# Two MLPs by a seven-product scheme: where the last additions into the residual happen, and where two groups of buffers lie

## The chip, the cores and the metric

The kernel runs on one core of a Trainium2 chip. The metric is device time in microseconds of one execution. Engines are named as the profile names them: PE is TensorE (matrix products, results in PSUM), DVE is VectorE, ACT is ScalarE, POOL is GpSimd, SP is SyncE. Each takes its instructions in order. SP issues most DMAs; the DMAs that add into their target are issued by POOL.

## The reference, cut to what matters

A residual stream x of 1024 tokens by 1024 channels goes through two layers and a last norm:

```
for l in range(2):
    h = rmsnorm(x, norm_mix_g[l])
    x = x + mixer(h)                       # l=0: attention and S5; l=1: HGRN2, 8 heads
    h = rmsnorm(x, norm_mlp_g[l])
    x = x + square(relu(h @ w_ff_in[l])) @ w_ff_out[l]     # 4096 hidden channels
return rmsnorm(x, final_norm_g)
```

The change is about the line with the MLP, and about the places of buffers in the two stages that follow or precede it.

## The kernel before, in words

**Products.** x is kept transposed, as eight tiles `x0` to `x7` of 128 channels by 1024 tokens. Each float32 operand is split into a high part (float32r, an ACT copy, L105) and the rest (a subtraction, L106), and a product is three matmuls: high by high, low by high, high by low (L349). A product of two matrices, each cut in 2 x 2 blocks, is made from seven block products in place of eight (`seven`, L334 on), in the order 1, 6, 5, 7, 2, 3, 4. They gather in three PSUM banks `a`, `b`, `c` (each there twice). Between them ACT copies `p1` from `a` (L355), and DVE makes `vv` and `ww` from `b` (L357, L359); a function `take` fetches the four result blocks after products 7, 2, 3 and 4. Products 7 and 4 go on gathering in `b` and product 3 in `c`, so PE may write them only when DVE has read what came before.

**First matmul of an MLP (`stage1`).** `entry` scales the eight x tiles by the norm's gain (ACT, L285), writes x to DRAM (`xd`, 16 blocks of 128x512, SP) and makes the seven right-hand sides of four pairs of tiles (`combos`: sums on DVE, L263 to L271, and splits). Each of the four goes to a slot: slots 0 to 3 are pools `t0` to `t3`, slot 4 is the place of the x tiles themselves, product p in the place of `x(p-1)`. Sixteen steps then make 256 hidden channels each and write them to DRAM (`spill`).

**Second matmul (`stage2`).** Its steps u run over bands of the hidden channels: step u multiplies up to four hidden blocks (rows u-4 to u-1 as far as they exist) into the pair of x tiles q, q+4 with q = (u - npairs) mod 4. npairs is 16 in the first MLP and 14 in the second, where the last four hidden tiles are left to `tail`. In the last four steps (u from npairs to npairs+3) 4, 3, 2 and 1 hidden blocks are left, and each finishes one pair of x tiles. Every step puts its four results into z tiles (one ACT copy, L434, and three DVE differences, L436) and adds them to `xd` in DRAM by POOL DMAs (L437). After each of the last four steps the pair is loaded back (`load_x`, L456). In the first MLP `fin` then squares the pair and adds the squares up (ACT L302, DVE L304) for the next norm; after the MLP the pair is scaled and split for the mixer (`new_xg`, L108 and L109). The block in slot 4 (rows 0, 5 and 10) is used last in step 14 of either MLP.

**Left sides (`left_sides`).** For each step SP loads four weight blocks `r11` to `r22` (L314), POOL makes three sums and a difference, ACT and DVE split seven of them into the rings `wh` and `wl`.

**Tail.** The second MLP's last four hidden tiles are loaded (L496) into eight z tiles, split, and multiplied plainly into each x tile (L527, L530); then come the last norm and the stores.

**Pools.** SBUF pools are stacked from either end. In an MLP: on the left `t2` and `pv` (the ring of the left sides: `r`, `s`, `wh`, `wl`, 46 KB per partition), on the right x, `t3`, `pe` (sums: eight z, `v`, `w`, `p1`, `ac`, `ad`, 26 KB), `t1`, `t0`. In the HGRN2 mixer: on the right x, `pgb`, `pgc`, `hgc` (kept small tiles: masks, `f`, `q`, `sc`), `pga`, `pw` (weights of the projections), on the left `hg` (its working tiles: `sn`, `oh`, `ol`, `M0`, `M1`, `on`, `qd0`, `ki0`, `qd1`, `ki1`, `V`, `sg`, `kT`). A tile that comes to lie over one of the stage before waits until that one has been read for the last time. Over `pw`, the mixer's weights of the last projections, lies `t0` in the second MLP.

**Order.** A planner puts each engine's instructions in an order at build time, by the order of the program as priority and by simulated times; waits between engines and for DMAs are then put in. On the chip an engine whose next instruction waits does not take a later one.

Of the kernel before, what the change touches and what calls it, by code (L numbers as in the profile page):

```python
# [10 lines left out]
F32 = mybir.dt.float32  # L11
# [3 lines left out]
ALU = mybir.AluOpType  # L15
# [4 lines left out]
P = 128  # L20
SEQ = 1024
# [34 lines left out]
class Trunk:  # L56
# [160 lines left out]

    def open_fast(self):
        self.st_f = [ExitStack() for _ in range(6)]
        t2, self.pv, t3, self.pe, t1, t0 = (  # L220
            st.enter_context(self.pool(n, side=side))
            for st, n, side in zip(
                self.st_f, ("t2", "pv", "t3", "pe", "t1", "t0"), ("left", "left", "right", "right", "right", "right")
            )
        )
        self.tp = (t0, t1, t2, t3)
        if self.ps_stack:
            self.ps_stack.close()
        self.ps_stack = ExitStack()
        self.ps_f, self.ps_sm = (  # L230
            self.ps_stack.enter_context(self.tc.tile_pool(name=n, bufs=2, space=PSUM, reuse_waits="tile"))
            for n in ("psx", "pss")
        )
# [189 lines left out]
        put(4, b21)  # L423
        return T

    def stage2(self, src, Ts, q):

        v, gp = self.nc.vector, self.nc.gpsimd
        (x11, x12), (x21, x22) = self.xd[q], self.xd[q + 4]

        def put(x, *src):
            t = self.z()
            if len(src) == 1:
                self.nc.scalar.copy(t, *src)  # L434
            else:
                v.tensor_tensor(t, *src, ALU.subtract)  # L436
            gp.dma_start(x, t, accum_op=ALU.add)  # L437

        def take(p, a, b, c, p1, vv, ww):
            if p == 7:  # L440
                put(x22, ww, c)
            elif p == 2:
                put(x11, a)
            elif p == 3:
                put(x12, c, vv)
            elif p == 4:
                put(x21, b, p1)

        self.seven(src, Ts, take)

    def load_x(self, q):
        out = []
# [7 lines left out]
    def mlp(self, l, Ts, fin=None):  # L460

        npairs = FF // 256 - 2 * l
        spill = [
            [self.pd.tile([P, 512], F32, tag=f"sq{j}{k}", name=f"sq{j}{k}") for k in range(4)] for j in range(FF // 256)
        ]
        rows = [self.stage1(l, Ts, spill)]
        xT = [None] * ND
        at = 0  # L470
        for u in range(1, npairs + 4):
            if u < npairs:
                rows.append(self.second_row(u, spill))
            use = range(max(0, u - 4), min(npairs, u))
            size = 4 * P * P * len(use)
            src = self.io[f"wout{l}"][at : at + size].rearrange("(k p c) -> k p c", k=4, p=P)
            at += size
            q = (u - npairs) % 4
            self.stage2(src, [rows[j] for j in use], q)
            if u >= npairs:  # L480
                xT[q], xT[q + 4] = self.load_x(q)
                if fin:
                    fin(q, xT)
        return xT, spill

    def tail(self, xT, spill):
# [448 lines left out]
    def attn_load(self, h, pa, qd, kd, dv):  # L935
        nc = self.nc
        st = []
        for c in range(2):
# [5 lines left out]
            st.append((qa, qb, kk))  # L944
        V = pa.tile([P, NT, P], F32, tag="V", name="V", bufs=2)
        nc.sync.dma_start(V.rearrange("p t c -> p (t c)"), dv[h])
        return dict(V=V, st=st)

# [286 lines left out]
    def hgrn_decay(self, h, d, gate, C, pt):  # L1235

        nc = self.nc
        v = nc.vector
        f, sn = gate
        om = C["om"][:, h : h + 1]  # L1240
        qd = pt.tile([P, SEQ], F32, tag=f"qd{d}", name=f"qd{d}", bufs=2 - d)
        ki = pt.tile([P, SEQ], F32, tag=f"ki{d}", name=f"ki{d}")
        blk = lambda t: t.rearrange("p (b s) -> p b s", b=NT)
        ones = self.ones[:, 0:64]

        near, far = (slice(64, 128), slice(0, 64)) if d == 0 else (slice(0, 64), slice(64, 128))
        qb, kb, fb = blk(qd), blk(ki), blk(f)
        for b in range(NT):
            if d == 0:
                v.tensor_tensor_scan(qb[:, b, 64:128], fb[:, b, 64:128], ones, 1.0, ALU.mult, ALU.mult)  # L1250
                v.tensor_tensor_scan(kb[:, b, 0:63][:, ::-1], fb[:, b, 1:64][:, ::-1], ones[:, 0:63], 1.0, ALU.mult, ALU.mult)
            else:
                v.tensor_tensor_scan(qb[:, b, 0:64][:, ::-1], fb[:, b, 0:64][:, ::-1], ones, 1.0, ALU.mult, ALU.mult)
                v.tensor_tensor_scan(kb[:, b, 65:128], fb[:, b, 64:127], ones[:, 0:63], 1.0, ALU.mult, ALU.mult)
        e = 63 if d == 0 else 64
        nc.gpsimd.memset(kb[:, :, e : e + 1], 1.0)

        dec = pt.tile([P, NT], F32, tag="dec", name="dec", bufs=4)
        nc.gpsimd.memset(dec, 0.0)
        if d == 0:  # L1260
            v.tensor_tensor(dec[:, 1:8], qb[:, 0:7, 127], kb[:, 1:8, 0], ALU.mult)
            v.tensor_tensor(dec[:, 1:8], dec[:, 1:8], fb[:, 1:8, 0], ALU.mult)
        else:
            v.tensor_tensor(dec[:, 0:7], qb[:, 1:8, 0], kb[:, 0:7, 127], ALU.mult)
            v.tensor_tensor(dec[:, 0:7], dec[:, 0:7], fb[:, 0:7, 127], ALU.mult)
        v.reciprocal(qb[:, :, far], kb[:, :, far])
        v.reciprocal(kb[:, :, near], qb[:, :, near])
        v.scalar_tensor_tensor(ki, sn, om, ki, ALU.mult, ALU.mult)
        return qd, ki, dec

    def hgrn_inputs(self, h, xg, C, pt):

        nc = self.nc
        v = nc.vector
        base = W_ODD + 5 * h
        load = lambda j: self.load_w(base + j, nc.gpsimd)
        H = {}
        g0 = self.hgrn_gate(h, load(1), xg, C, pt)
        yield H
        g1 = self.hgrn_gate(h, load(2), xg, C, pt)  # L1280
        yield H
        d0 = self.hgrn_decay(h, 0, g0, C, pt)
        ps = self.proj(load(3), xg)
        t = pt.tile([P, SEQ], F32, tag="sn", name="t", bufs=2)
        v.tensor_tensor(t, ps, self.R, ALU.mult)
        yield H
        d1 = self.hgrn_decay(h, 1, g1, C, pt)
        ps = self.proj(load(0), xg)
        q = self.pc1.tile([P, SEQ], F32, tag="q", name="q")
        v.tensor_tensor(q, ps, self.R, ALU.mult)  # L1290
        V = pt.tile([P, SEQ], F32, tag="V", name="V")
        self.to_tokens(t, lambda j: slice(128 * j, 128 * j + 128), V, lambda p: p)
        H["V"] = V
        H["dirs"] = [d0, d1]
        for d in (d0, d1):
            v.tensor_tensor(d[0], d[0], q, ALU.mult)
        yield H
        ps = self.proj(load(4), xg)
        sg = pt.tile([P, SEQ], F32, tag="sg", name="sg")
        v.tensor_tensor(sg, ps, self.R, ALU.mult)  # L1300
        nc.scalar.activation(sg, sg, AF.Sigmoid)
        H["sg"] = sg
        yield H

    def hgrn_mix(self, h, H, C, pt):

        nc = self.nc
        v, gp = nc.vector, nc.gpsimd
        wide = lambda tag, bufs=1: pt.tile([P, SEQ], F32, tag=tag, name=tag, bufs=bufs)
        dirs, V = H["dirs"], H["V"]  # L1310
        sc = self.pc1.tile([P, NT, P], F32, tag="sc", name="sc")
        for g in range(2):
            gs = slice(4 * g, 4 * g + 4)
            for d in range(2):
                qd, ki, dec = dirs[d]
# [7 lines left out]
        for d in range(2):  # L1323
            kT = wide("on" if d else "kT")
# [125 lines left out]
@with_exitstack  # L1450
def trunk_kernel(ctx, tc, io):
    T = Trunk(ctx, tc, io)
    ctx.callback(lambda: T.ps_stack.close())
    nc = T.nc
    v = nc.vector
    T.setup()

    def load_xT():
        T.px = ctx.enter_context(T.pool("px", side="right"))
        out = []  # L1460
        for d in range(ND):
            t = T.px.tile([P, SEQ], F32, tag=f"x{d}", name=f"x{d}")
            nc.sync.dma_start(t, io["x"][d])
            out.append(t)
        return out

    mix, xT = T.mixer0(load_xT)
    for _ in T.out_proj(0, mix, PAIRED, xT):
        pass
    T.st_b.close()  # L1470
    T.st_w.close()
    T.st_m.close()
    T.open_fast()
    Ts = T.entry(xT, 16, (0, 1, 2, 3))
    acc = []

    def fin(q, x):
        if q == 0:
            acc.extend(T.half(t) for t in ("ac", "ad"))
        for d in (q, q + 4):  # L1480
            T.square_add(acc, x[d], d == 0, T.z)

    xT, _ = T.mlp(0, Ts, fin)
    T.finish_rstd(T.pc, acc)
    T.close_fast()
    T.open_hgrn()
    xg = [None] * ND
    for d in PAIRED:
        xg[d] = T.new_xg(d, xT[d], T.gcol(8, d))
    T.psum(3, 0, 2)  # L1490
    T.mixer1(xg, xT)
    T.close_hgrn()
    T.open_fast()
    Ts = T.entry(xT, 24, (1, 3, 0, 2))
    xT, spill = T.mlp(1, Ts)
    T.tail(xT, spill)

# [86 lines left out]
```

## Time and profile before

| | us |
|---|---|
| median of 3 runs | 2767.81 (2761.88 to 2770.64) |
| the profiled execution | 2766.7 |
| its span in the profile | 2764.9 |
| PE busy | 2550.8 (92%) |
| DVE busy | 1999.2 (72%) |
| ACT busy | 1059.9 (38%) |
| POOL busy | 958.1 (35%) |

The stages, from the first and last matmuls of their lines: attention and S5 mixer to 641, first MLP 641 to 1349, HGRN2 mixer 1349 to 2033, second MLP 2036 to 2685, tail from 2697. Busy time of PE is that of pipelined matmuls; what is of use is where it is idle and what ended the idle time. The granted clock (PEclk) is a share of full speed.

### The profile page before, as it was taken

The numbers are of one execution on the slowest core, as the hardware profiler recorded it, in microseconds if no ns is written. First come the engines' busy times: TensorE is split into PE (matmuls) and PEld (weight loads), VectorE is DVE, ScalarE is ACT, GpSimd is POOL, SyncE is SP. The second block draws the span as 40 slices with busy tenths as digits, with TensorE's granted clock in tenths as the row PEclk, the third lists the DMA queues.
The fourth block names the chain that finished last, engine by engine and source line by source line (L and its number), as shares of the span: only waits on it lengthen the run. The fifth ranks groups of instructions, "written<-read, shape, count | busy, mean of one in ns | idle before, by whom it ended". The sixth has DMA issues, their size and how long they took to land.

```text
span 2764.9 us, 33375 instructions
## 1 busy us (share of the span) xinstructions
PE 2550.8 (92%) x12040; PEld 2080.2 (75%) x12040; DVE 1999.2 (72%) x2868; ACT 1059.9 (38%) x1918; POOL 958.1 (35%) x759
## 2 busy tenths in 40 slices
PE   6888889998999989999799999999879999899977
PEld 5676768885788857787588888888757888677756
DVE  9788867767667678886485767666586676688845
ACT  3233346655334344443322122222163343444424
POOL 6555421231323234454222222222233232345432
PEclk8989999999999999999799999999989999999998
DMA  3222452321334257566411011111033332567672
GB/s 142 65 84 72 143 148 66 88 80 50 99 107 125 93 148 177 143 176 138 92 54 39 32 45 39 39 39 39 16 107 98 109 122 96 146 154 174 142 171 101
DMA packets 139285, 276.36 MB, mean 100 GB/s; under 512 B 16880, under 2 KB 29808, under 8 KB 139120
## 3 DMA queue, kind: packets, MB, share of 16 engines
q1 hardware_dynamic: 118384, 236.47, 26.8%
q0 software_dynamic: 20736, 37.76, 8.8%
q8 instruction: 95, 1.56, 0.2%
q14 instruction: 70, 0.57, 0.1%
HBM read 173.50 MB, written 94.37 MB: 97 GB/s over the span
## 4 chain that ended last, share of the span: by engine, by line
PE 65%; DVE 15%; issue 7%; DMA 6%; POOL 3%; ACT 2%; SPq 1%; POOLq 0%; DVEq 0%; ACTq 0%
PE big L130 19%; PE b L349 14%; PE c L349 9%; PE a L349 9%; DMA z<-sq 3%; DVE wl L106 2%; PE sm L995 2%; DVE l L106 2%; PE big L1363 1%; PE sm L130 1%; PE tail L527 1%; PE big L960 1%; PE sm L1319 1%; PE big L1334 1%; PE big L961 1%
## 5 line engine op out<-in xcount | busy, mean ns | idle before, releaser
L130 PE MATMUL big<-hi,wh 128*128 128x512 f32 x976 | 312.8, 401 | 12.8 <-ACT hi L108 11.3
L130 PE MATMUL big<-lo,wh 128*128 128x512 f32 x976 | 309.5, 396 | 9.4 <-DVE lo L109 9.4
L130 PE MATMUL big<-hi,wl 128*128 128x512 f32 x976 | 310.1, 398 | 0.0
L349 PE MATMUL b<-h,wh 128*128 128x512 f32 x672 | 271.7, 404 | 30.7 <-DVE w L359 29.4
L349 PE MATMUL b<-l,wh 128*128 128x512 f32 x672 | 269.5, 401 | 2.3 <-DVE l L106 2.3
L349 PE MATMUL b<-h,wl 128*128 128x512 f32 x672 | 269.2, 401 | 1.0 <-DVE wl L106 1.0
L105 ACT CAST wh<-s 128x512 fp32r<-128x512 f32 (+3 forms) x204 | 118.4, 583 | 356.4 <-PE b L349 160.0
L106 POOL TENSOR_TENSOR wl<-raw,wh 128x1024 fp32r<-128x1024 f32 x58 | 143.2, 2468 | 305.4 <-ACT wh L105 305.3
L105 ACT CAST wh<-raw 128x1024 fp32r<-128x1024 f32 x74 | 77.5, 1048 | 441.5 <-PE big L130 296.6
L106 DVE TENSOR_TENSOR wl<-r,wh 128x512 fp32r<-128x512 f32 (+3 forms) x279 | 220.1, 797 | 24.7 <-ACT wh L105 24.4
L106 DVE TENSOR_TENSOR l<-z,h 128x512 fp32r<-128x512 f32 x232 | 191.7, 856 | 60.5 <-ACT h L105 60.1
L130 PEld LDWEIGHTS big<-lo,wh 128*128 128x128 f32 x976 | 184.8, 190 | 52.1 <-DVE lo L109 11.1
L130 PEld LDWEIGHTS big<-hi,wh 128*128 128x128 f32 x976 | 182.8, 191 | 52.4 <-ACT hi L108 12.0
L437 POOL DMA_DIRECT2D xd<-z x144 | 127.6, 971 | 272.5 <-ACT z L434 181.0
L130 PEld LDWEIGHTS big<-hi,wl 128*128 128x128 f32 x976 | 185.6, 191 | 40.4 <-issue 0.2
L105 ACT CAST wh<-r 128x512 fp32r<-128x512 f32 (+3 forms) x279 | 159.8, 582 | 123.3 <-PE b L349 60.6
L105 ACT CAST h<-z 128x512 fp32r<-128x512 f32 x232 | 139.0, 620 | 170.0 <-DMA z<-sq 62.1
L349 PE MATMUL a<-h,wh 128*128 128x512 f32 x448 | 181.3, 405 | 14.7 <-ACT p L355 6.3
L323 POOL TENSOR_TENSOR s<-s,r 128x512 f32<-128x512 f32 (+3 forms) x68 | 107.0, 1573 | 244.4 <-DVE wl L106 243.3
L106 DVE TENSOR_TENSOR wl<-s,wh 128x512 fp32r<-128x512 f32 (+3 forms) x204 | 138.7, 681 | 71.5 <-ACT wh L105 68.2
L349 PE MATMUL c<-h,wh 128*128 128x512 f32 x448 | 180.2, 402 | 8.6 <-ACT h L105 5.4
L349 PE MATMUL a<-h,wl 128*128 128x512 f32 x448 | 180.7, 403 | 4.3 <-DVE wl L106 4.3
(430 smaller groups left out, 6007.2 us busy)
## 6 DMA issues: line engine op xcount, KB each, us to landing
raw<-w SPq DMA_DIRECT2D x74, 512.0 KB, 3.3
xd<-z POOLq DMA_DIRECT2D x144, 256.0 KB, 5.8
r<-win SPq DMA_DIRECT2D x128, 256.0 KB, 2.9
sq<-z SPq DMA_DIRECT2D x128, 256.0 KB, 2.9
z<-sq SPq DMA_DIRECT2D x128, 256.0 KB, 4.9
r<-wout SPq DMA_DIRECT2D x96, 256.0 KB, 4.6
x<-x SPq DMA_DIRECT2D x16, 512.0 KB, 6.6
xd<-x SPq DMA_DIRECT2D x32, 256.0 KB, 2.3
```

The source lines that it names most:

```text
L105: nc.scalar.copy(hi, src)
L106: (eng or nc.vector).tensor_tensor(lo, src, hi, ALU.subtract)
L130: nc.tensor.matmul(ps[:, t], a[:, s], b[:, t], start=(first and i == 0 and j == 0), stop=(last and i == n - 1 and j == 2),)
L323: gp.tensor_tensor(s2, s1, r["r11"], ALU.add)
L349: nc.tensor.matmul(bank[p], x[:, s], y, start=(p in (1, 6, 5) and i == 0 and j == 0), stop=(i == n - 1 and j == 2), skip_group_check=True,)
L437: gp.dma_start(x, t, accum_op=ALU.add)
L527: nc.tensor.matmul(ps, x[:, ks], y, start=(k == 0 and j == 0), stop=(k == 3 and j == 2))
L960: nc.tensor.matmul(S[:, ks], qa[:, qs], kk[:, ks], start=True, stop=False)
L961: nc.tensor.matmul(S[:, ks], qb[:, qs], kk[:, ks], start=False, stop=True)
L995: nc.tensor.matmul(po, wT[:, k, :], A["V"][:, k, :], start=(k == 0), stop=(k == NT - 1))
L1319: nc.tensor.matmul(ps[:, 128 * b : 128 * b + 128], ki[:, bs], qd[:, bs], start=True, stop=True)
L1334: nc.tensor.matmul(kv[:, bs], kTs[d][:, bs], V[:, bs], start=True, stop=True)
```

## The change

The last four steps of the first MLP and the last three of the second add their seven pieces to the x tiles in SBUF, on DVE, with seven additions or subtractions in place of three differences, a copy and four adding DMAs. For this the x tiles are loaded before: in the first MLP pair k before step npairs - 1 + k, in the second pairs 1 to 3 before step npairs - 2 + k, while its pair 0 still goes through DRAM in step npairs and is loaded after step npairs + 1.

In an MLP the pools `pv` and `pe` change places: `pv` lies on the right between `t3` and `t1`, `pe` on the left after `t2`. In the mixer the tiles `qd1`, `ki1`, `V`, `sg` and `kT` (4 KB each) move from `hg` on the left to `hgc` on the right. And the four pairs of the second MLP's entry go to slots 0, 3, 1, 2 in place of 1, 3, 0, 2.

```diff
     def open_fast(self):
-        t2, self.pv, t3, self.pe, t1, t0 = (
+        t2, self.pe, t3, self.pv, t1, t0 = (
...
-                self.st_f, ("t2", "pv", "t3", "pe", "t1", "t0"), ("left", "left", "right", "right", "right", "right")
+                self.st_f, ("t2", "pe", "t3", "pv", "t1", "t0"), ("left", "left", "right", "right", "right", "right")
...
-    def stage2(self, src, Ts, q):
+    def stage2(self, src, Ts, q, x=None):
...
-        self.seven(src, Ts, take)
+        def take_here(p, a, b, c, p1, vv, ww):
+            x11, x12, x21, x22 = (x[k // 2][:, 512 * (k % 2) : 512 * (k % 2) + 512] for k in range(4))
+            for y, plus, minus in {7: [(x22, ww, c)], 2: [(x11, a, None)], 3: [(x12, c, vv)], 4: [(x21, b, p1)]}.get(p, []):
+                v.tensor_tensor(y, y, plus, ALU.add)
+                if minus is not None:
+                    v.tensor_tensor(y, y, minus, ALU.subtract)
+
+        self.seven(src, Ts, take_here if x else take)
...
-            self.stage2(src, [rows[j] for j in use], q)
-            if u >= npairs:
-                xT[q], xT[q + 4] = self.load_x(q)
-                if fin:
-                    fin(q, xT)
+            for k in {npairs - 1: (0,), npairs: (1,), npairs + 1: (2,), npairs + 2: (3,)}.get(u + l, ()):
+                if l == 0 or k:
+                    xT[k], xT[k + 4] = self.load_x(k)
+            here = xT[q] is not None and u >= npairs
+            self.stage2(src, [rows[j] for j in use], q, [xT[q], xT[q + 4]] if here else None)
+            if u == npairs + 1 and l:
+                xT[0], xT[4] = self.load_x(0)
+            if u >= npairs and fin:
+                fin(q, xT)
...
-        qd = pt.tile([P, SEQ], F32, tag=f"qd{d}", name=f"qd{d}", bufs=2 - d)
-        ki = pt.tile([P, SEQ], F32, tag=f"ki{d}", name=f"ki{d}")
+        pool = self.pc1 if d else pt
+        qd = pool.tile([P, SEQ], F32, tag=f"qd{d}", name=f"qd{d}", bufs=2 - d)
+        ki = pool.tile([P, SEQ], F32, tag=f"ki{d}", name=f"ki{d}")
...
-        V = pt.tile([P, SEQ], F32, tag="V", name="V")
+        V = self.pc1.tile([P, SEQ], F32, tag="V", name="V")
...
-        sg = pt.tile([P, SEQ], F32, tag="sg", name="sg")
+        sg = self.pc1.tile([P, SEQ], F32, tag="sg", name="sg")
...
-        wide = lambda tag, bufs=1: pt.tile([P, SEQ], F32, tag=tag, name=tag, bufs=bufs)
+        wide = lambda tag, bufs=1: (self.pc1 if tag == "kT" else pt).tile([P, SEQ], F32, tag=tag, name=tag, bufs=bufs)
...
-    Ts = T.entry(xT, 24, (1, 3, 0, 2))
+    Ts = T.entry(xT, 24, (0, 3, 1, 2))
```

## Rows read from the trace of the kernel before

**Rows 1.** The page, part 1: busy us (share of the span) and instructions.

```profile
PE 2550.8 (92%) x12040; PEld 2080.2 (75%) x12040; DVE 1999.2 (72%) x2868; ACT 1059.9 (38%) x1918; POOL 958.1 (35%) x759
```

**Rows 2.** Windows: stretch, length, busy of PE, PEld, DVE, ACT, POOL, PEclk, DMA.

```profile
1278.00:1298.00 20.00, 20.00 (x87) 15.95 (x85) 10.06 (x17) 5.84 (x12) 8.07 (x10) 1.00 0.54 92
1298.00:1348.60 50.60, 30.90 (x95) 21.72 (x95) 27.33 (x40) 20.86 (x38) 16.68 (x18) 0.76 0.68 152
1348.60:1378.80 30.20, 25.62 (x111) 21.48 (x110) 13.92 (x54) 6.13 (x10) 5.56 (x20) 0.83 0.40 72
1378.80:1985.00 606.20, 605.08 (x3175) 513.42 (x3174) 416.72 (x627) 134.51 (x229) 163.39 (x102) 1.00 0.12 39
...
2646.00:2685.50 39.50, 31.29 (x121) 22.85 (x119) 18.52 (x35) 12.09 (x28) 14.59 (x19) 0.96 0.84 181
2685.50:2697.30 11.80, 0.02 (x1) 0.03 (x1) 2.63 (x5) 1.31 (x3) 2.10 (x3) 0.68 1.08 295
```

**Rows 3.** Timeline of PE, end of the first MLP: start, length, instruction, [idle before <-releaser].

```profile
1330.10 0.80 PE L349 MATMUL b<-h,wh 128*128 128x512 f32 x1 [4.93 <-DVE w L359]
...
1345.86 0.80 PE L349 MATMUL b<-h,wh 128*128 128x512 f32 x1 [6.24 <-DVE w L359]
...
1363.32 2.04 PE L152 MATMUL sm<-ones,ac 128*128 128x128 f32 x8 [4.58 <-DVE ex L568]
```

**Rows 4.** Timeline of ACT, in the same stretch.

```profile
1343.85 1.15 ACT L302 ACTIVATE z<-x 128x512 f32<-128x512 f32 x2 [6.59 <-DMA x<-xd]
```

**Rows 5.** Waits of SP's queue: waited for: us in total, times, longest.

```profile
SPq L456 <- DMA xd<-z: 86.2, 29, 9.3
```

**Rows 6.** DMA issues: count, KB each, median us from issue to landing.

```profile
xd<-z POOLq DMA_DIRECT2D x144, 256.0 KB, 5.8
...
x<-xd SPq DMA_DIRECT2D x32, 256.0 KB, 3.3
```

**Rows 7.** Lines, DVE, 1298 to 1378.8: count, busy us, mean ns, idle before.

```profile
L304 DVE TENSOR_TENSOR ac<-ac,z 128x512 f32<-128x512 f32 x7 | 4.8, 688 | 13.4 <-ACT z L302 13.4
L304 DVE TENSOR_TENSOR ad<-ad,z 128x512 f32<-128x512 f32 x7 | 4.8, 687 | 4.9 <-ACT z L302 4.9
L436 DVE TENSOR_TENSOR z<-b,p 128x512 f32<-128x512 f32 x4 | 2.7, 680 | 0.0
```

**Rows 8.** Timeline of DVE, end of the first MLP.

```profile
1302.15 2.40 DVE L106 TENSOR_TENSOR wl<-r,wh 128x256 fp32r<-128x256 f32 x1 [3.20 <-ACT wh L105]
...
1348.11 0.69 DVE L304 TENSOR_TENSOR ac<-ac,z 128x512 f32<-128x512 f32 x1
1348.72 0.69 DVE L304 TENSOR_TENSOR ad<-ad,z 128x512 f32<-128x512 f32 x1
```

**Rows 9.** Timeline of POOL, in the same stretch.

```profile
1301.89 2.38 POOL L106 TENSOR_TENSOR wl<-raw,wh 128x1024 fp32r<-128x1024 f32 x1 [1.70 <-ACT wh L105]
```

**Rows 10.** Timeline of PE, end of the second MLP and the tail's start.

```profile
2662.30 0.63 PE L349 MATMUL b<-h,wh 128*128 128x512 f32 x1 [2.86 <-DVE w L359]
...
2697.28 0.79 PE L527 MATMUL tail<-h,h 128*128 128x512 f32 x1 [11.83 <-ACT h L105]
2697.87 0.63 PE L527 MATMUL tail<-h,l 128*128 128x512 f32 x1
2698.29 0.63 PE L527 MATMUL tail<-h,wh 128*128 128x512 f32 x1
```

**Rows 11.** Timeline of ACT, end of the second MLP.

```profile
2659.96 0.62 ACT L105 CAST h<-r 128x512 fp32r<-128x512 f32 x1 [4.23 <-DMA r<-wtail]
...
2696.61 1.79 ACT L105 CAST h<-z 128x512 fp32r<-128x512 f32 x3 [5.38 <-DMA z<-sq]
```

**Rows 12.** Timeline of PE, start of the second MLP.

```profile
2036.47 0.50 PE L349 MATMUL a<-h,wh 128*128 128x512 f32 x1 [3.02 <-ACT wh L105]
2040.73 0.80 PE L349 MATMUL a<-h,wl 128*128 128x512 f32 x1 [3.75 <-DVE wl L106]
```

**Rows 13.** Lines, DVE, 2009 to 2033: count, busy us, mean ns, idle before.

```profile
L106 DVE TENSOR_TENSOR l<-z,h 128x512 fp32r<-128x512 f32 x10 | 6.4, 681 | 0.0
```

## Prediction, made before the changed kernel was seen

> **What bounds the kernel now.** I read part 1 of the page first: TensorE is busy for 92% of the span [rows 1], so a change pays only where TensorE waits or runs at its lower clock. Busy times by stretch then show where that is [rows 2]. In the long odd-layer mixer, 1378.8 to 1985 us, TensorE is busy 605.1 of 606.2 us. In the four products of the last pairs of the first MLP and the start of the mixer (1298 to 1378.8) it is busy 56.5 of 80.8 us, at a mean clock of 0.76 and 0.83. From 2646 to 2697.3, the last three pairs of the second MLP, it is busy 31.3 of 51.3 us. These two ends, and the start of the second MLP, are the places that the diff touches. The rest should stay.
>
> In the first end the reader is to see one pattern in TensorE's timeline three times: idle 4.93 and 6.24 us until VectorE has made `w` (L359), and 4.58 us before the norm's sums [rows 3]. VectorE makes `w` late because it takes its instructions in order and the square sums (L304) stand in front: they wait for ScalarE, which waited 6.59 us for the reload of x (`x<-xd`) [rows 4]. In that stretch VectorE stood 13.4 and 4.9 us before the two sums [rows 7]. The reload is late because it waits on SyncE for the adding DMA to land: 86.2 us in 29 waits [rows 5], and such a DMA takes 5.8 us, the reload 3.3 us more [rows 6]. So each of the last pairs goes PSUM, z, adding DMA, reload, square, and the other engines' queues stand behind it.
>
> In the second end the same SyncE waits hold back the loads queued behind them: TensorE stands 2.86 us, because a split of the tail's weights waits for `r<-wtail` in front of `w`, and then 11.83 us until ScalarE has the first activation [rows 10], for which ScalarE waited on `z<-sq` [rows 11].
>
> **Part 1: the last pairs are added in SBUF.** Removed: the four z copies or differences of 7 pairs (4 in the first MLP, 3 in the second; the second's first pair stays with DRAM, as its x is not loaded yet) and 28 of 144 adding DMAs. Per pair ScalarE loses one copy, VectorE gets 7 additions in place of 3 differences. The reloads stay 32 in number, but are issued one pair ahead, at a time when the last addition into that x lies three pairs back.
>
> First end. TensorE's work from 1298 to 1378.8 is 95 matmuls, then 111 of which 32 are the small ones of the norm. At full clock one costs 20.0 us / 87 = 0.23 us [rows 2]; eight small ones took 2.04 us [rows 3], the other sixteen about 2. The floor is (95 + 79) x 0.23 + 4 + 2 = 46 us, 35 less than now. VectorE comes first, though. It is busy 27.3 + 13.9 = 41.2 us there [rows 2]. The change adds 3 pairs x 4 additions and 2 for the end of the pair before, 14, at 0.60 us from start to start [rows 8]: 8.4 us, so 49.6 us, to 1347.6 if it never idles. The last `lo` (L109) must come before the last 24 matmuls of the first projection and the norm's 32: with what TensorE can do meanwhile that puts it at about 1352 where it now stands at 1378.8, 27 less. Some idling stays, since with one or two blocks a product is shorter than the copy, difference and additions around it. For its size I take the second end, where three such pairs leave TensorE idle 39.5 - 31.3 - 2.86 = 5.3 us that are not due to a load [rows 2, 10]. So **22 us**. From above 27. From below: only the 18.3 us before L304 go and the 8.4 us come on top: 10.
>
> The order of the seven sets another small wait. After product 7 TensorE may not write bank `c` before VectorE has read it; now that is one difference, afterwards the addition of `ww` stands ahead of it: 0.6 us more per pair, inside the 5.3 us kind above.
>
> Second end. TensorE's floor from 2646 is 119 x 0.23 = 27 us. VectorE is busy 18.5 + 2.6 us [rows 2]; 12 more additions are 7.2 us and the eight splits of the tail's activations, which now come after 2697, move in with 5.3 us: 33.6 us, to 2679.6. The tail then starts 17.7 us earlier, and its first 14 matmuls, now at the lower of the two clock levels (0.43 us from start to start [rows 10]), gain 14 x 0.20 = 2.8 us if there is no gap in front: 20.5. With 5 us of idling left: **16 us**. From below: only the 11.83 us and the 2.8 go, the 7.2 come: 7. Late next is VectorE's own queue, not a transfer: the z ring is no longer used by the last three pairs, so `z<-sq` can be issued while they run, and no SyncE wait for an adding DMA stands in front. After the tail's start TensorE is steadily busy up to the last norm, so what is won there reaches the end.
>
> A rule of the Trainium skill speaks against this part. The rows: a split of 128x256 took 2.40 us (1302.15), beside a 2.38 us subtraction of GpSimd that began 0.26 us before it [rows 8, 9]. The page SBUF — State Buffer (Who interferes with whom) says that a VectorE instruction with two SBUF inputs contends with a GpSimd instruction that reads SBUF, and that the loser waits for the whole instruction. Three of the seven additions (`ww`, `vv`, `p1`) have both inputs in SBUF, the differences that they replace had one in PSUM. By the rule, with GpSimd busy 16.7 of 50.6 us, a third of 21 additions would wait up to 2 us: 14 us, and the sum would be 2742. But the square sums L304 also have two SBUF inputs, and 14 of them in that stretch average 0.688 us against 0.680 us for L436, which reads PSUM [rows 7]. I keep 0.60 us.
>
> **Part 2: the places in SBUF.** At the start of the second MLP the ring of split weights (`pv`) now lies over the mixer's q and k products, which are read until its last mixing step; afterwards it lies over masks, gates and scores, read earlier. So the first weights can be loaded and split before TensorE needs them, and the 3.02 us (ScalarE's `wh`) and 3.75 us (`wl`) in front of the first two matmuls [rows 12] can go: +7. Against that the blocks' places change: (1,3,0,2) to (0,3,1,2) puts the first block into slot 0, which in both layouts lies over the mixer's projection weights, and TensorE reads these to its last projection, at 2033. Before that VectorE now does 10 splits [rows 13] and 7 sums; the first block would be stuck after its first split, with five of the eight z's, and so the second block as well. About 10 of these 17 instructions then come after 2033, 6 us in a stretch where VectorE is the last to finish. I take **+2**, from -6 to +7. At the start of the first MLP two of the seven `wl` now lie over the mixer output that the last projection reads: two splits late, **-1** (-2 to 0). In the mixer every tile keeps its size and count, only the pool differs, and TensorE has no idle time there to lose or win: 0. GpSimd's 28 issues and ScalarE's copies are off the path: 0.
>
> **Sum.** 22 + 16 + 2 - 1 = 39 us. The profiled execution took 2766.7 us (span 2764.9), 1.1 below the median of 2767.8, so I forecast 2766.7 - 39 = 2728 us. From below 10 + 7 - 6 - 2 = 9 (2758), from above 27 + 20.5 + 7 = 54.5 (2712). Its own range is 2714 to 2741.
>
> **Rivals.**
> - VectorE takes the place of the DMA. All 26 added VectorE instructions lie in stretches where it is the last, and the first block of the second MLP is stuck as above. Then the sums come near their lower ends, some 12 us: 2755 (2742 to 2759). For it: the floors above are VectorE's, not TensorE's. Against: its idle time in the first end is 80.8 - 41.2 = 39.6 us, five times what is added. Chance 0.2.
> - Slower: the wait moves onto VectorE. Its first addition of a pair waits for the reload, and the splits and `w` that TensorE needs stand behind it in order, as behind L304 now. If the reload lands after product 7 of its pair, the stalls stay, and 26 x 0.6 = 16 us come on top: 2782. It decides where the reload is less than about 8 us ahead (5.8 + 3.3). For it: three of the second MLP's reloads need the place of block 10, which the pair before still reads, and SyncE waits in order. Against: from that block's second-last use to the addition lie some 14 us of products. Chance 0.06.
> - More: with no waits left, both ends reach their floors and the second MLP starts without its two gaps: 2712 (2700 to 2714). VectorE would have to be without idle time. Chance 0.08.
> - Nothing: the stalls were set by the order in which instructions were planned, and the new plan has others of the same size, 2767 (2759 to 2775). Against: the waits named end on a transfer, not on an order. Chance 0.04.
>
> **How the numbers follow.** The forecast has 0.62. The range 2712 to 2750 holds it, half of the first rival and a part of the third, about 0.8. A measurement can tell 0.3% (8.3 us) from no change. Faster than 2759.5: 0.62 + 0.2 + 0.08 = 0.90. Same 0.04, slower 0.06.
>
> **What would show it.** Right: no SyncE wait on an adding DMA in the last pairs; no ScalarE wait for `x<-xd` before a square; TensorE's idle time between 1298 and the first gate down from 24 to under 10 us; the 11.83 us before the tail gone; the mixer still about 606 us; 116 adding DMAs. Wrong: an addition in SBUF that begins after a reload lands with TensorE idle behind it; the mixer longer by more than 3 us; or at the second MLP's start VectorE's queue ending later than now by more than 6 us.

## The result and the profile after

The changed kernel takes 2722.4 us (median of 4 runs, 2720.0 to 2727.5) where the kernel before takes 2765.2: ratio 0.9846, 95% interval 0.9821 to 0.987. The profiled execution took 2724.6 us (span 2722.8). The forecast was 2728. Its sum was right to 3 us, but not its terms, as this table shows. It cuts both spans at the same matmuls, counted from the start of each stage. The third column is the forecast, the rest are the differences to the kernel before (us), each from one profiled execution; "additions only" and "places only" are the runs with one part of the change each.

```
stretch (in the trace before)                    length  forecast  changed  additions only  places only
start to stage 2 of the first MLP, 0-983.4        983.4      +1      -5.8        +0.6          -5.1
steps 1 to 14 of stage 2, 983.4-1251.2            267.8       0      -0.5        +0.6          -1.2
steps 15 and 16, 1251.2-1290.4                     39.2       0      +5.2        +6.2          -0.7
steps 17 to 19, mixer's start, 1290.4-1378.8       88.4     -22     -16.4       -15.5          -3.2
the mixer, 1378.8-2033.1                          654.3       0      -0.9        +0.5          +0.9
start of the second MLP, 2033.1-2104.2             71.1      -2      -2.7        +0.9          -4.0
rest of its stage 1, 2104.2-2380.2                276.1       0      -5.1         0.0          -5.2
steps 1 to 14 of its stage 2, 2380.2-2644.6       264.3       0      -0.1        -0.4          -4.7
step 15 to the end, 2644.6-2764.9                 120.3     -16     -15.7       -15.1          -2.9
sum                                                         -39     -42.0       -22.2         -26.1
```

Three rows carry what was not foreseen: 11 us gained in the two rows with a stage 1, where the change adds and removes no instruction, and 5 us lost in steps 15 and 16. The page, part 1, beside [rows 1]: VectorE has 28 instructions more, GpSimd 28 fewer, as counted.

```profile
PE 2527.8 (93%) x12040; PEld 2077.1 (76%) x12040; DVE 2018.5 (74%) x2896; ACT 1055.8 (39%) x1911; POOL 921.4 (34%) x731
```

The windows, beside [rows 2] (stretch, length, busy time of PE, PEld, DVE, ACT, POOL with instructions, granted clock, DMA share, GB/s): first end, mixer, the last steps before the tail's first matmul, and the rest of those steps.

```profile
1289.30:1361.30 72.00, 58.13 (x236) 44.84 (x235) 59.06 (x118) 29.98 (x48) 14.66 (x25) 0.88 0.13 44
1361.30:1967.00 605.70, 604.56 (x3174) 513.41 (x3173) 411.84 (x621) 130.03 (x225) 160.62 (x101) 1.00 0.13 41
2618.20:2650.10 31.90, 25.52 (x97) 19.42 (x95) 18.75 (x36) 10.98 (x25) 6.16 (x9) 0.89 0.81 246
2650.10:2674.00 23.90, 22.75 (x96) 17.77 (x97) 17.87 (x30) 8.35 (x15) 0.00 (x0) 1.00 0.11 34
```

TensorE's timeline in the first end has no 4.93, 6.24 and 4.58 us any more [rows 3]. In their place stand short waits for VectorE, in each of the last two pairs for `v` and for `w`.

```profile
1305.77 0.49 PE L349 MATMUL a<-h,wh 128*128 128x512 f32 x1 [1.83 <-ACT wh L105]
...
1319.42 0.50 PE L349 MATMUL b<-h,wh 128*128 128x512 f32 x1 [2.87 <-DVE v L357]
1323.82 0.80 PE L349 MATMUL b<-h,wh 128*128 128x512 f32 x1 [2.29 <-DVE w L359]
...
1332.47 0.50 PE L349 MATMUL b<-h,wh 128*128 128x512 f32 x1 [2.58 <-DVE v L357]
1336.07 0.80 PE L349 MATMUL b<-h,wh 128*128 128x512 f32 x1 [2.64 <-DVE w L359]
```

VectorE's timeline ahead of the second of these (`w`, 1323.09) shows why. Nothing in it is idle; what TensorE waits for stands at the end of a queue of splits and square sums.

```profile
1318.69 0.68 DVE L357 TENSOR_TENSOR v<-b,p 128x512 f32<-128x512 f32 x1
1319.29 0.28 DVE L106 TENSOR_TENSOR wl<-r,wh 128x128 fp32r<-128x128 f32 x1
1319.49 0.68 DVE L304 TENSOR_TENSOR ad<-ad,z 128x512 f32<-128x512 f32 x1
1320.09 0.68 DVE L304 TENSOR_TENSOR ac<-ac,z 128x512 f32<-128x512 f32 x1
1320.69 1.27 DVE L109 SCALAR_TENSOR_TENSOR lo<-x,vec,hi 128x1024 fp32r<-128x1024 f32 x1
1321.89 0.68 DVE L304 TENSOR_TENSOR ad<-ad,z 128x512 f32<-128x512 f32 x1
1322.49 0.68 DVE L304 TENSOR_TENSOR ac<-ac,z 128x512 f32<-128x512 f32 x1
1323.09 0.68 DVE L359 TENSOR_TENSOR w<-b,p 128x512 f32<-128x512 f32 x1
```

SyncE's waits for an adding DMA, 86.2 us in 29 before [rows 5], are halved, not gone; 116 adding DMAs are left of 144 [rows 6].

```profile
SPq L464 <- DMA xd<-z: 49.4, 15, 8.0
```

At the second end the 2.86 and 11.83 us [rows 10] are replaced by one 4.70 and one 1.46, and the tail's first products now run between the last pairs' own.

```profile
2637.58 0.51 PE L349 MATMUL a<-h,wh 128*128 128x512 f32 x1 [4.70 <-ACT wh L105]
2639.55 0.80 PE L349 MATMUL b<-h,wh 128*128 128x512 f32 x1 [1.46 <-DVE w L359]
2647.71 0.49 PE L349 MATMUL a<-h,wh 128*128 128x512 f32 x1 [0.18 <-ACT p L355]
2650.14 0.49 PE L539 MATMUL tail<-h,h 128*128 128x512 f32 x1
```

### The profile page after: what moved, and what is told of

The parts are those of the page before. It is cut to its first block, busy times and chain, and to the rows that moved or that the text cites. A ratio compares the mean times of both kernels' runs of the same rounds, so it can differ in the third digit from the quotient of the medians.

```text
span 2722.8 us, 33307 instructions
## 1 busy us (share of the span) xinstructions
PE 2527.8 (93%) x12040; PEld 2077.1 (76%) x12040; DVE 2018.5 (74%) x2896; ACT 1055.8 (39%) x1911; POOL 921.4 (34%) x731
## 4 chain that ended last, share of the span: by engine, by line
PE 60%; DVE 20%; DMA 8%; issue 6%; ACT 2%; POOL 2%; SPq 1%; POOLq 0%; DVEq 0%; ACTq 0%
PE big L130 21%; PE b L349 11%; PE c L349 7%; PE a L349 7%; DMA z<-sq 5%; DVE wl L106 3%; DVE l L106 3%; PE sm L1007 2%; PE sm L130 1%; PE big L1376 1%; PE tail L539 1%; PE big L972 1%; PE sm L1332 1%; PE big L1347 1%; DMA xd<-z 1%
## 5 line engine op out<-in xcount | busy, mean ns | idle before, releaser
L323 POOL TENSOR_TENSOR s<-s,r 128x512 f32<-128x512 f32 (+3 forms) x68 | 98.7, 1452 | 255.1 <-DVE wl L106 254.0
L349 PE MATMUL c<-l,wh 128*128 128x512 f32 x448 | 177.1, 395 | 4.4 <-DVE l L106 4.4
L330 POOL TENSOR_TENSOR s<-s,r 128x512 f32<-128x512 f32 (+3 forms) x68 | 88.8, 1305 | 273.1 <-DVE wl L106 217.4
```

What stands on the lines that cost most here:

```text
L323: gp.tensor_tensor(s2, s1, r["r11"], ALU.add)
L330: gp.tensor_tensor(s2, s2, r["r12"], ALU.add)
L349: nc.tensor.matmul(bank[p], x[:, s], y, start=(p in (1, 6, 5) and i == 0 and j == 0), stop=(i == n - 1 and j == 2), skip_group_check=True,)
```

## The experiments

The runs after a point are made to answer it; each is the changed kernel with the edit shown, unless it says "the kernel before". Ratios are to the kernel before, timed on the same chip; the changed kernel has 0.9846.

### 1 and 2: the two parts apart

```diff
# additions only: the kernel before with stage2 and mlp of the changed kernel
# places only: the changed kernel with stage2 and mlp of the kernel before
```

> The kernel before with the additions in SBUF and the earlier reloads alone; pools and block places as before. Theory (the adding DMA out of the queues is what pays, at the first and the second end): 31 of the 42 us come, 16 at the first end and 15 before the tail, so 2766 - 31 = 2735 us (2730 to 2740). Rival (the places in SBUF bring most of it, by letting loads start earlier): 2750 us or more. In the trace, by the theory, the 11.83 us before the tail and the waits of ScalarE for the reload are gone as after the whole change.

> The changed kernel with the additions put back into DRAM and the reloads back behind their pair; pools and block places stay changed. Theory: only the start and the first stage of the second MLP gain, 3 + 5 us, and the two ends stand as before: 2766 - 8 = 2758 us (2754 to 2763). Rival (places bring most): 2740 us or less. Nothing (places alone do nothing): 2766.

Measured: additions only 2745.0 us, 0.9934 (0.9918 to 0.995); places only 2742.9 us, 0.9926 (0.9907 to 0.9945). Both expectations were wrong, the theory's and the rival's. Each part brings about half, and within the intervals the two add up to the whole. The additions bring 15 us at either end, as in the whole change, and lose 6 us in steps 15 and 16. The places bring 5 us in each row with a stage 1, 5 in the second MLP's stage 2, and 3 to 4 at the start and the ends. So the places act also where TensorE never waits.

The windows of one such stretch say how. These are 740 to 930 us, the first MLP's stage 1, of the kernel before, additions only, places only and the changed kernel. TensorE is busy for all 190.00 us at full granted clock in each, and does 817, 816, 830 and 830 matmuls.

```profile
740.00:930.00 190.00, 190.00 (x817) 153.06 (x816) 130.45 (x185) 73.88 (x123) 55.39 (x38) 1.00 0.38 114
```

```profile
740.00:930.00 190.00, 190.00 (x816) 153.18 (x816) 130.47 (x186) 73.88 (x123) 55.94 (x38) 1.00 0.38 114
```

```profile
740.00:930.00 190.00, 190.00 (x830) 155.53 (x829) 132.09 (x189) 74.53 (x125) 56.55 (x39) 1.00 0.37 116
```

```profile
740.00:930.00 190.00, 190.00 (x830) 155.43 (x829) 132.11 (x188) 74.81 (x126) 57.30 (x39) 1.00 0.38 114
```

The same matmuls follow each other faster: 233.2 ns apart before, 229.3 after (means of all starts under 245 ns apart in both MLPs). A pair here is one step: seven products of four blocks, three matmuls each, 84 in all. The intervals repeat to 1 or 2 ns from pair to pair at the same place in the pair. Matched with the addresses of the compiled program, which stand in no trace, they go with where the operands lie: 226 or 227 ns for most where weights and moving block (the activations that stream past them) both lie on the right, mostly 231 to 238 where they lie on different sides. Two things differ between the sides: the region, and the start. Tiles on the left start at a multiple of 128 B, those on the right 96 B past one. The pads of runs 5, 6, 7 and 9 below bear the difference of 96 B out.

### 3 and 4: two steps of the prediction

```diff
-    Ts = T.entry(xT, 24, (0, 3, 1, 2))
+    Ts = T.entry(xT, 24, (1, 3, 0, 2))
```

> The changed kernel with the order of block places (1,3,0,2) instead of (0,3,1,2) at the entry of the second MLP. The prediction's step (the first block in place 0 waits for the last projection's weights and costs up to 6 us): about 2718 us, with splits of the first block before the last projection ends. Rival (the splits come late because the plan puts them behind the last addition to x, whatever their place): 2721 to 2725 us, no change. Third (place 0 for the first block is the better one in the new layout): 2728 us or more.

Measured: 2723.9 us, 0.9856 (0.9834 to 0.9878). The order of places makes no difference that can be told: the start of the second MLP (the row of 71.1 us) is 2.8 us shorter than before, 2.7 in the changed kernel.

```diff
-            for k in {npairs - 1: (0,), npairs: (1,), npairs + 1: (2,), npairs + 2: (3,)}.get(u + l, ()):
-                if l == 0 or k:
-                    xT[k], xT[k + 4] = self.load_x(k)
+            if u >= npairs and (l == 0 or q):
+                xT[q], xT[q + 4] = self.load_x(q)
```

> The changed kernel with each reload of x written directly ahead of the pair that adds into it, in place of one pair ahead (second MLP: its first pair still through DRAM). It prices the rival that turned on the reload being late. If the reload has to be about 8 us ahead, its first addition stands and with it the splits behind it: 2735 us or more, with VectorE waiting for the reload. If SyncE gets to it early enough anyway, as nothing stands in front of it: 2721 to 2727 us, no such wait.

Measured: 2723.3 us, 0.9848 (0.9827 to 0.987), no change, and steps 15 and 16 as long as in the changed kernel. Where the reload stands in the code hardly matters: the order written out by the planner brings it ahead either way. So this run does not price a late reload; the slower rival was not tried in its own form.

### 5, 6, 7 and 9: phase or region

```diff
         self.pc = pool("const")
+        pad = pool("pad", side="right")
+        self.pad = pad.tile([P, 24], F32, tag="pad", name="pad")
```

This is the pad of 96 B on the right (5), the same in the kernel before (7), and with 8 in place of 24 the pad of 32 B (9). For 6 the tile of 96 B is taken from `self.pc`, on the left.

> The changed kernel with a 96 B pad under the top of SBUF, so that every tile on the right begins 96 B lower and on the same multiple of 128 B as those on the left; no tile changes its region, size or count. In the trace of the places-only run a pair of 84 matmuls takes 19.28 us where it took 19.58, at full granted clock and with TensorE never idle, and the interval from one matmul to the next repeats to 1 ns per place in the pair: 226 or 227 ns where weights and moving block both lie on the right, 231 to 238 ns where one lies left and one right. Left tiles begin at a multiple of 128 B, right ones 96 B past one. Theory A (the phase of weights and moving block against each other sets the interval): all come to about 227 ns, a pair to 19.05 us, 5208 x 2.5 ns = 13 us less than the changed kernel: 2709 us (2704 to 2714). Rival B (the region, near or far, left or right, sets it): 2722, no change. Rival C (a right tile off 128 B is what is fast): slower, up to 233 ns, 2742 us.

> The changed kernel with a 96 B pad among the constants, so that the left tiles begin 96 B past a multiple of 128 B as the right ones do: all in one phase, none on the multiple. Theory A (equal phase is enough): as with the pad on the right, 2709 us (2704 to 2714). Theory A' (the multiple of 128 B itself counts): 2722 or slower, up to 2742. Rival B (region): 2722.

> The kernel before with the 96 B pad on the right, nothing else. Its weights lie left and three of its four block places right. Theory A: 5208 x (233.2 - 227) ns = 32 us less than before, so 2766 - 32 = 2734 us (2728 to 2740), more than all of what the moved places give (21 us) and with no tile in another region. Rival B (region): 2766, no change. Rival C: slower than 2766.

> The changed kernel with a pad of 32 B instead of 96 B on the right: right tiles begin 64 B past a multiple of 128 B, left tiles on it. With 96 B between the two sides a steady pair of 84 matmuls took 19.28 us (changed kernel), with 0 B between them 19.04 us (both pads of 96 B). If the phase counts modulo 64 B, a pair takes 19.04 us and the whole 2717 us. If it counts modulo 128 B or more, a pair takes 19.2 us or more and the whole 2722 us or more. The pair's time is the measure, the whole differs by little more than can be told.

The phase of a tile is what is left of its start address after whole multiples of 128 B. Measured, with the time of a steady pair of 84 matmuls (start to start, repeated to 0.03 us over ten pairs) in the first and second MLP:

```
kernel                   tiles start, past 128 B   ring of    pair of 84, us   median   ratio (interval)
                            left      right        weights    first   second
before                        0         96          left      19.58   19.59    2765
additions only                0         96          left      19.58   19.59    2745.0   0.9934 (0.9918 to 0.995)
places only                   0         96          right     19.28   19.22    2742.9   0.9926 (0.9907 to 0.9945)
changed                       0         96          right     19.28   19.22    2722.4   0.9846 (0.9821 to 0.987)
9: changed, pad 32 right      0         64          right     19.33   19.30    2724.5   0.986 (0.9839 to 0.9881)
5: changed, pad 96 right      0          0          right     19.04   19.04    2717.2   0.9821 (0.9808 to 0.9834)
6: changed, pad 96 left      96         96          right     19.04   19.04    2717.4   0.983 (0.9817 to 0.9843)
7: before, pad 96 right       0          0          left      19.04   19.04    2743.6   0.9924 (0.9908 to 0.9941)
```

The windows of 740 to 930 us of run 5 and of run 7 have 840 matmuls each.

```profile
740.00:930.00 190.00, 190.00 (x840) 157.36 (x839) 134.42 (x190) 75.78 (x127) 58.89 (x40) 1.00 0.36 115
```

```profile
740.00:930.00 190.00, 190.00 (x840) 157.40 (x840) 134.41 (x191) 76.07 (x127) 58.78 (x40) 1.00 0.35 116
```

It is the phase. With one phase on both sides a pair takes 19.04 us wherever the ring lies, on the multiple of 128 B or 96 B past it; 64 B apart is as slow as 96. Run 7 gains with 96 unused bytes what the moved places gain (0.9924 and 0.9926). The move works because it brings the ring to the side of three of the four block places; before, it shared its side with one. Why two phases cost TensorE some 6 ns a matmul in the kernel before (233.1 against 226.7 on the mean) is not shown by these runs. Nor is it a matter of each matmul alone: taken in the order of the program, the one block that lies on the ring's side in the kernel before comes at 224 to 238 ns, 232.4 on the mean, the other three at means of 232.8 to 233.9 (first MLP).

As whole times, 5 and 6 are not clear of the changed kernel, nor are 8 and 11 below: their intervals overlap with 0.9821 to 0.987. What these four show is read from the stretches of their traces; run 7 is clear of the kernel before.

The size missed in 5, 6 and 7: 13 and 32 us were expected, 5 and 22 came. The first stages gained in full: in run 5 they take 10.7 and 7.6 us less than before, 7.0 and 7.2 of it in 13 steady pairs each (0.54 and 0.55 us a pair). The second ones gained nothing. The windows of steps 1 to 14 of the first MLP's second stage are those of the kernel before and of run 5: the same matmuls in the same time, with 13.9 us idle and the clock at 0.99 before, 17.4 us and 0.97 in run 5. What the faster matmuls win there is lost again in waits and at the lower clock after them. Of the waits in run 5 most are for `w` (7.0 us, 4.4 before) and for splits by ScalarE (4.0 and 1.7).

```profile
983.40:1251.20 267.80, 253.89 (x1051) 197.56 (x1050) 223.32 (x304) 123.47 (x219) 123.27 (x107) 0.99 0.64 160
```

```profile
969.10:1237.50 268.40, 251.00 (x1052) 200.53 (x1051) 216.31 (x298) 121.22 (x216) 122.80 (x107) 0.97 0.66 166
```

### 8 and 10: VectorE at the ends

```diff
+            if p == 1:
+                gp.tensor_tensor(x22, x22, p1, ALU.subtract)
+            elif p == 6:
+                v.tensor_tensor(x12, x12, b, ALU.subtract)
+                gp.tensor_tensor(x12, x12, p1, ALU.add)
+                gp.tensor_tensor(x21, x21, p1, ALU.subtract)
+            elif p == 7:
+                v.tensor_tensor(x22, x22, b, ALU.add)
+                v.tensor_tensor(x22, x22, c, ALU.subtract)
+            elif p in (2, 3, 4):
+                y, z = {2: (x11, a), 3: (x12, c), 4: (x21, b)}[p]
+                v.tensor_tensor(y, y, z, ALU.add)
```

> The changed kernel with the last pairs' p1 added to x by GpSimd (three instructions of 128x512 per pair) and v and w dropped: 6 VectorE instructions per pair in place of 9. Theory (VectorE's queue is what is late at the first end, 26.46 us busy of 29 from 1316 to 1345): 3 pairs x 3 x 0.65 = 6 us less there, little at the second end: 2716 us (2713 to 2720). Rival (GpSimd, 1.4 to 1.8 us for such an instruction, becomes late in the short pairs, or it holds up VectorE's instructions with two SBUF inputs): 2722 or slower.

> Both that pay by themselves: the 96 B pad on the right and p1 added by GpSimd. The pad gave 5 us and GpSimd's additions 6 us against the changed kernel. If they add up (one lies in the matmul rate everywhere, the other at the two ends): 2711 us (2708 to 2714). If the faster matmuls only make VectorE and the weights late sooner: 2716 us, as either alone.

Measured: 8, 2716.6 us, 0.9823 (0.981 to 0.9835); 10, with the 96 B pad on the right as well, 2702.2 us, 0.9777 (0.9758 to 0.9797). Steps 17 to 19 and the mixer's start are 25.4 us shorter than before in run 8 and 25.6 in run 10, against 16.4, so these instructions on VectorE had cost 9 us there. That is more than the 6 us expected of nine instructions fewer: the edit also drops `v` and `w`, the two results that TensorE waited for (5.5 and 5.6 us in the changed kernel), and no run separates the two. TensorE is busy 56.55 of 62.90 us, with 54.00 us of VectorE and 27.67 of GpSimd beside it, and its waits for `v` and `w` are gone (waits of PE, the same stretch: us in total, times, longest).

```profile
1291.20:1354.10 62.90, 56.55 (x236) 43.54 (x235) 54.00 (x109) 29.76 (x48) 27.67 (x35) 0.92 0.15 49
```

```profile
PE c L349 <- DVE x L460: 3.1, 2, 1.9
PE b L349 <- ACT z L302: 2.3, 2, 2.1
PE c L349 <- ACT wh L105: 0.7, 1, 0.7
```

Run 10 beats both kernels, and by 9 us more than was expected; steps 1 to 14 of the second MLP's second stage, which differ by some us from plan to plan, are 6.2 us shorter than before in it, 0.1 in the changed kernel. In run 8 steps 15 and 16 take 9.9 us more than before (5.2 in the changed kernel), in run 10 only 4.1, so run 8 alone keeps about half of its 9 us. These are differences of single traces.

### 11 and 12: the wait in step 15

The 5 us lost in steps 15 and 16 come with reloads that SyncE holds up. Its waits from 1236 to 1256 us in the changed kernel are the first row; behind them in its queue stand the loads of weights and spilled blocks. TensorE's window of step 15 is the second: 84 matmuls in 24.4 us, 2.8 us idle and at a mean clock of 0.93, where places only took 19.2 (third). Its one long wait there, 2.1 us (the granted clock is 0.71 from 1250 to 1255), ends at 1251.2 on `w`, which VectorE makes behind the splits of a spilled block; SyncE issued the loads of that block from 1236.1 on, after a wait of 2.5 us in front of a reload. The wait of 8.0 us ends at 1246.7, and the next load of weights goes out at 1251.8, too late to be the cause of that stall. So the rows show that the queue is held, not which of the waits costs how much; run 11 takes all of them out of SyncE's queue.

```profile
SPq L464 <- DMA xd<-z: 10.4, 2, 8.0
```

```profile
1245.00:1269.40 24.40, 21.57 (x86) 16.73 (x85) 15.12 (x23) 9.58 (x18) 8.48 (x8) 0.93 0.71 184
```

```profile
1244.90:1264.10 19.20, 19.20 (x86) 15.78 (x84) 16.44 (x22) 8.65 (x15) 9.35 (x8) 1.00 0.67 151
```

```diff
-                self.nc.sync.dma_start(x[:, 512 * k : 512 * k + 512], self.xd[d][k])
+                self.nc.gpsimd.dma_start(x[:, 512 * k : 512 * k + 512], self.xd[d][k])
```

> The changed kernel with the reloads of x issued by GpSimd in place of SyncE. In the changed kernel step 15 of the first MLP's second stage takes 24.4 us, with places alone 19.2: SyncE waits up to 8.0 us in front of a reload for the adding DMA of the pair before, and the weight loads stand behind it. Theory (that wait is what holds up TensorE there): step 15 comes down to about 19.5 to 20.5 us, the whole to 2718 us (2714 to 2721). Rival (GpSimd now waits in the same way, and its sums for the weights stand behind it, or the step is long for another reason): step 15 stays at 23 us or more, the whole at 2722 or above.

Measured: 2717.5 us, 0.9831 (0.9808 to 0.9854). Step 15 takes 20.9 us, steps 15 and 16 together 1.0 us more than before instead of 5.2. GpSimd now waits for the same DMAs, 13.4 us in 9 from 1225 to 1300, but what stands behind it seems to be needed later than the loads; that is not tested. In the seven other traces with both parts and the reloads on SyncE (3 to 6, 8 to 10) step 15 takes 23.6 to 25.4 us, in the two with the reloads on GpSimd (11 and 12) 20.9.

```profile
1248.00:1268.90 20.90, 19.45 (x85) 15.68 (x84) 18.05 (x23) 9.20 (x16) 11.75 (x13) 1.00 0.81 202
```

> The 96 B pad, p1 added by GpSimd and the reloads issued by GpSimd, all three. In the run with the first two step 15 of the first MLP still takes 24.0 us, against 20.9 us with the reloads on GpSimd alone. If these 3 to 4 us add up: 2698.5 us (2696 to 2701). If GpSimd, which now adds and waits for the reloads, is late in the last pairs: 2702 us or more, with step 18 above the 11.9 us that it takes without.

Measured: 2708.0 us, 0.9808 (0.9792 to 0.9825): not better than run 10. Step 15 falls from 24.0 to 20.9 us as hoped, but step 17 rises from 15.6 to 19.7, not step 18 (11.9 in both). GpSimd does the last steps' additions, reloads and weight sums in one queue; in it two additions of step 17 stand ahead of a sum (L329) for its weights.

```profile
1280.92 1.31 POOL L455 TENSOR_TENSOR x<-x,p 128x512 f32<-128x512 f32 x1
1282.18 1.29 POOL L459 TENSOR_TENSOR x<-x,p 128x512 f32<-128x512 f32 x1
1283.42 0.73 POOL L329 TENSOR_TENSOR r<-r,r 128x256 f32<-128x256 f32 x1
```

In step 17 TensorE then waits for weights, `wl` and `wh`, where run 10 has neither (waits of PE in run 12).

```profile
PE b L351 <- DVE wl L108: 1.4, 1, 1.4
PE b L351 <- ACT wh L107: 1.2, 1, 1.2
PE b L351 <- DVE x L461: 0.7, 1, 0.7
```

So the two cures share one engine. That the rise comes from there alone is read from this queue, not tested by a run.

## Why the prediction came out as it did

That the time was right is luck: two errors cancel, 11 us too much at the first end and 11 us not seen in the rows with a stage 1.

- **Second end, 16 forecast, 15.7 measured.** The mechanism held: the 11.83 us went, and the tail's first products moved in between. The reason "`z<-sq` can be issued while they run" held too, but not "no SyncE wait for an adding DMA stands in front": SyncE waits 3.6 us for one ahead of a reload at 2627.2, and the first `z<-sq` goes out behind that, at 2627.6. ScalarE waits 5.9 us for it, and that is the 4.70 us left.
- **First end, 22 forecast, 16.4 measured, 11.2 with what it cost ahead.** The stalls behind the reload went. The step that failed is the size of the idling left, taken from the second end as 5.3 us; 13.9 us are left (11.1 of them waits for `v` and `w`), as VectorE has the mixer's splits (`lo`) and the square sums in its queue beside the additions. "From 24 to under 10 us" was wrong for the same reason. Runs 8 and 10 bear it out: with `v`, `w` and nine of VectorE's instructions gone, 9 us come back in this stretch.
- **"No SyncE wait on an adding DMA in the last pairs" was wrong.** The prediction reckoned that an x is reloaded three pairs after its last addition. The planner brings the reloads forward until they wait again, 49.4 us in all, and later loads stand behind them. Run 11 shows 4 us of price in steps 15 and 16 (one trace against one). What was asked of every moved step, which queue it is moved past, was not worked out for the reload.
- **Part 2, start of the second MLP, 2 forecast, 2.7 measured, in part for the reason given.** The gain that was named came: TensorE's waits of 3.02 us for `wh` and 3.75 us for `wl` are gone in the changed kernel and with places only, and stand with additions only. The loss set against it was laid to the slot order (-6), which was worth nothing: in the changed kernel TensorE waits 5.3 us for ScalarE's splits `h` of the blocks and 2.5 for VectorE's `l`, with the old order (run 3) 6.0 and 2.5.
- **"The rest should stay" was wrong.** "Every tile keeps its size and count, only the pool differs" was said of the mixer and held there (605.7 against 606.2 us). To the two first stages the prediction gave nothing (-1 at the start of the first), as TensorE is never idle there. But there the address counts: 0.30 and 0.37 us a pair, 3.9 and 4.9 us in the 13 steady pairs of each MLP. Runs 5, 6, 7 and 9 show that it is the phase.
- **Rivals.** "VectorE takes the place of the DMA" describes the first end, but not the second nor the price it named. The slower rival, VectorE held up by a late reload, did not come: no addition of the last pairs waits for a reload, they wait for TensorE's products. (Its lead of "about 8 us" should be the 9.1 us of 5.8 + 3.3.)
- **The rule on VectorE and GpSimd** (the Trainium skill, SBUF — State Buffer, Who interferes with whom). The additions cost what was taken, 0.69 us long and 0.60 from start to start; GpSimd is busy for only 14.66 of the 72.00 us there. For the splits the trace agrees with the rule: beside GpSimd's long subtractions two of 128x256 last as long as these, 2.33 and 2.62 us, and 0.41 alone. The rows are VectorE's and then GpSimd's timeline in the changed kernel. That 0.60 us came out right because the two engines' work hardly met is read from these rows, not tested.

```profile
1298.22 2.33 DVE L106 TENSOR_TENSOR wl<-r,wh 128x256 fp32r<-128x256 f32 x1
1301.35 2.62 DVE L106 TENSOR_TENSOR wl<-r,wh 128x256 fp32r<-128x256 f32 x1
1304.48 0.41 DVE L106 TENSOR_TENSOR wl<-s,wh 128x256 fp32r<-128x256 f32 x1
```

```profile
1297.87 2.41 POOL L106 TENSOR_TENSOR wl<-raw,wh 128x1024 fp32r<-128x1024 f32 x1
...
1300.84 2.84 POOL L106 TENSOR_TENSOR wl<-raw,wh 128x1024 fp32r<-128x1024 f32 x1
```

## What to carry to other kernels

Before a bound engine's time is taken as given, divide its busy time by its instructions in a steady stretch of both kernels: a change of tile addresses alone can show up as busy time, at full clock, in no wait. For float32r products like these, keep the start addresses of weights and moving data in one phase (modulo 128 B) on both sides of SBUF; a pad of 96 B was worth 22 us here, as much as the reordering of the pools. A load moved forward is moved past what its queue waits for, so price the in-order queue behind it, and split the part of a sum that needs no PSUM off to an idle engine only as long as that engine has no other new duty.

## What the hardware showed that was not expected

- A matmul of 128x512 at full clock followed the one before by 226.7 ns (19.04 us / 84) with all operands in one phase modulo 128 B, and in the first MLP by 229.5 (19.28 / 84) and 233.1 (19.58 / 84) with the ring of weights in the phase of three and of one of the four block places, 96 B from the rest.
- 64 B apart (19.33 us a pair) was no better than 96 B (19.28), so 64 B is not the period; whether it is 128 B or a multiple was not tried, nor were other distances than 0, 64 and 96 B.
